# FFN down product as seven half-size block products, with operand sums formed in the up stage

## The chip, the cores and the metric

The kernel runs on one core of a Trainium2 chip. The metric is the time of the whole kernel on the device in microseconds. The engines of the core are named as in the profile: PE (TensorE, the matrix engine; PEld is its loading of the stationary operand), DVE (VectorE), ACT (ScalarE), POOL (GpSimd) and SP (SyncE, which here issues nearly all DMA transfers).

## The reference

One decoder layer on 1024 tokens and 16 prepended meta tokens, model width 1024. Behind two token mixers comes the feed-forward part, which this change is about. Cut to what matters:

```python
D_MODEL, SEQ, D_FF, FFN_TAPS = 1024, 1024, 2816, 3

h = layer_norm(DEEPNORM_ALPHA * h + mixed @ w_out, ln1_g, ln1_b)
up = causal_dwconv(h @ ffn_w_up, ffn_dw, ffn_dw_b)
u, g = jnp.split(up, 2, axis=-1)
f = (jax.nn.gelu(g, approximate=False) * u) @ ffn_w_down
return layer_norm(DEEPNORM_ALPHA * h + f, ln2_g, ln2_b)
```

Everything is in float32. The last product, the down product, takes the 1024 x 2816 result of the gate and the 2816 x 1024 weight `ffn_w_down`.

## The kernel before, in words

**Precision.** Every matrix operand is split into a rounded part `hi` (a cast on ScalarE, line 1042, 317 or 1203) and the rest `lo` (a subtraction on VectorE, line 1043, 320 or 1204). A product is three matmuls: hi x hi, hi x lo, lo x hi. The stationary operand is 128x128, the moving one up to 512 columns wide, and the result goes to one of eight PSUM banks.

**Up stage (about 664 to 1084 us).** It runs over `FC` = 22 chunks of 128 gate channels and the 128 value channels that belong to them. Each turn already uses seven block products in place of eight for the product with `w_up` (line 1139): names B11, B21, BT2, BT4, BT1, BT3 and B22, 24 matmuls each, into four double banks `pw`, `px`, `pz`, `py`. The sums on the activation side stand in memory for the whole stage; the sums on the weight side are formed per turn (lines 1064 to 1070) and split into a ring of ten slots (`RING`), up to nine products ahead (`w_ahead(9)`). The results leave PSUM by copies on ScalarE (line 1151) and additions on VectorE (line 1147): `c11` from `pz`, `c22` and `c21` behind the sixth product, `c12` from `py` behind the seventh. `u13`, `u2` and `c22` are work rows in `OB`. Then come the convolution of three taps (lines 1100 to 1102), the gelu and the product of gate and value (line 1110). The 128x1024 result of a turn is stored to DRAM as `fd[c]`, in two halves of 512 tokens.

**Down stage (from 1084 us).** It loads `fd` and `w_down` back, splits them, and multiplies: two passes over 512 tokens each, all 22 chunks of 128 in a pass, in blocks of 2, then 4 chunks; in a block four row tiles of 128 tokens and two halves of 512 output columns, three matmuls per chunk (line 1239). The eight banks of a pass accumulate over the whole pass. The weight is loaded and split once per pass. Landing places: eight ring slots in `FA` (`ftmp`) for `fd`, two buffers `wr` for the weight. In block 14 the residual rows are loaded from `h1d` and prepared (lines 1228 and 1229). With the last block each row tile gets its two banks added (line 1242), then the layer norm: statistics (229, 233), square root on ScalarE (236), a few one-column steps (237 to 245), scaling (1249, 1250) and two stores to the output.

**What sets the order.** Instructions of an engine run in the order of its queue. A scheduler writes the queues: `rank(p)` sets an instruction's priority (lower goes first), `after(a, b)` puts `a` behind `b` in the queue, and waits between engines come from the data. Transfers issued with `load` stand in SP's queue in order; a transfer that must wait for its data holds up those behind it.

Of the kernel before, what the change touches and what calls it, by code (L numbers as in the profile page):

```python
# [29 lines left out]
P = 128  # L30
# [14 lines left out]
FC = DFF // P  # L45
NB = S // P
# [52 lines left out]
def tile_hybrid_layer(  # L99
# [55 lines left out]


# [61 lines left out]
    def ln_stats(srcs, pool=None, tag="", bufs=4, behind=None):  # L218
# [7 lines left out]
        for j, (src, m) in enumerate(srcs):  # L226
            st = small.tile([P, 2, 6], F, name="st")
            for i in range(2):
                ins = nc.vector.bn_stats(st[:m, i, :], src[:, i * 512:(i + 1) * 512])
# [562 lines left out]
    RX = rx_p.tile([P, 4096], R, name="RX")  # L792
# [235 lines left out]
    ps_stack.close()  # L1028
    up_stack = ExitStack()
# [79 lines left out]
    def f_out(c, h, gate, t):  # L1109
        nc.vector.tensor_tensor(t, t, gate, OP.mult)  # L1110
        load(fd[c, :, h * 512:(h + 1) * 512], t)

    last_mm, copied = [], []
    RK_CHAIN = 400
    with rank(RK_SPLIT):
        w_ahead(7)
    for c in range(FC):
        V4, X, Z, Y = (pup.tile([P, 1024], F, name=n, tag=n) for n in ("pw", "px", "pz", "py"))
        passes = ((1,), (0,)) if c == 0 else ((0, 1),)
        for subs in passes:  # L1120
# [24 lines left out]
            def tt(*x):  # L1145
                with rank(RK_CHAIN):
                    nc.vector.tensor_tensor(*x)
# [7 lines left out]
            prod(B21, Z, True)  # L1155
            tt(c11[:, a:b], at(Z), u13[:, a:b], OP.add)
# [13 lines left out]
            tt(c22[:, a:b], c22[:, a:b], u13[:, a:b], OP.add)  # L1170
# [14 lines left out]
    g1, b1, g2, b2_ = (dn.tile([P, D], F, name=n) for n in ("g1", "b1", "g2", "b2"))  # L1185
    for i, t in enumerate((g1, b1)):
        load(t, dram(ln1_in, i * D, [[0, P], [1, D]]))
    for i, t in enumerate((g2, b2_)):
        load(t, dram(ln2_in, i * D, [[0, P], [1, D]]))
    nc.vector.tensor_scalar(b1, b1, ALPHA, None, OP.mult)  # L1190

    w_dn_v = w_down.rearrange("(k p) c -> k p c", p=P)
    FS = [(RX, i * 1024) for i in range(4)] + [(RHO, i * 1024) for i in range(8)]
    WS = [(t, i * 2048) for t in (OC, RHC) for i in range(4)]
    fs_n, wd_n = [0], [0]

    def f_chunk(c, s):
        raw = ftmp()
        load(raw, fd[c, :, s * 512:(s + 1) * 512])
        t, o = FS[fs_n[0] % len(FS)]  # L1200
        fs_n[0] += 1
        hi, lo = t[:, o:o + 512], t[:, o + 512:o + 1024]
        nc.scalar.copy(hi, raw)
        nc.vector.tensor_tensor(lo, raw, f32(hi), OP.subtract)  # L1204
        return hi, lo

    def wd_chunk(c):
        raw = wraw([P, D])
        load(raw, w_dn_v[c])
        t, o = WS[wd_n[0] % len(WS)]  # L1210
        wd_n[0] += 1
        hi, lo = t[:, o:o + 1024], t[:, o + 1024:o + 2048]
        split(raw, hi, lo, True)
        return hi, lo

    BLOCKS = [range(0, 2)] + [range(a, a + 4) for a in range(2, FC, 4)]
    BANKS = (2, 3, 4, 5, 0, 1, 6, 7)
    for s in range(2):
        banks = [pdn.tile([P, 512], F, name="ps_d", tag=f"d{j}") for j in range(8)]
        rows = []  # L1220
        for cs in BLOCKS:
            ops = [f_chunk(c, s) + wd_chunk(c) for c in cs]
            first, last = cs[0] == 0, cs[-1] == FC - 1
            if cs[0] == 14:
                for i in range(4):
                    r = dn.tile([P, D], F, name="r", tag="r", bufs=4)
                    load(r, h1d[(s * 4 + i) * P:(s * 4 + i + 1) * P, :])
                    nc.vector.scalar_tensor_tensor(r, r, ALPHA, g1, OP.mult, OP.mult)
                    nc.vector.tensor_tensor(r, r, b1, OP.add)
                    rows.append(r)  # L1230
# [74 lines left out]
```

## Time and profile before

| | us |
|---|---|
| three runs, median (lowest, highest) | 1341.49 (1341.06, 1342.19) |
| the profiled execution's own time | 1339.96 |
| its span, first to last instruction | 1338.1 |
| up stage, from the first full turn | about 664 to 1083.9 |
| down stage on TensorE | 1083.87 to 1327.94 |
| from TensorE's last matmul to the end | 10.16 |

The page gives the busy time of each engine and its share of the span. A window row gives the same for a stretch. A timeline row is one or several equal instructions: start, length, engine, line, what is written and read, and in brackets how long the engine stood idle before and what ended that. A group row is all instructions of one line and shape: busy time, mean nanoseconds of one, idle time in front of them and its releasers. Durations of neighbours on an engine overlap a little, so the distance of starts is shorter than the duration. L12 is line 12 of the kernel that the row belongs to; the change shifts lines, so the same instruction has other numbers before and after.

### The profile page before, as it was taken

How to read it: one execution, taken by the hardware profiler on the slowest of the kernel's cores; microseconds unless marked ns; L12 is line 12 of the kernel's file. 1: busy time of each engine (PE TensorE's matmuls, PEld its weight loads, DVE VectorE, ACT ScalarE, POOL GpSimd, SP SyncE). 2: the span in 40 equal slices, each digit the busy share in tenths (PEclk: the TensorE clock that was granted, in tenths of full speed). 3: DMA queues.
4: the chain of work that ended last, by engine and by line, in shares of the span. 5: the costliest groups of instructions: out<-in, count | busy, mean ns of one | idle time of the engine just before them, and what ended most of it. 6: DMA issues, size and time to landing. Idle time of an engine off the chain costs nothing.

```text
span 1338.1 us, 21743 instructions
## 1 busy us (share of the span) xinstructions
PE 1305.2 (98%) x8646; PEld 1215.2 (91%) x8646; DVE 1015.0 (76%) x1759; ACT 574.0 (43%) x1047; POOL 70.0 (5%) x43
## 2 busy tenths in 40 slices
PE   6999999999999999999899999999999999999996
PEld 5999999999999999878899999999999988888885
DVE  8689899999969576466988778778778784468417
ACT  4522244545473223344655555555555553323310
POOL 1300000010112231000000000000000000000000
PEclk9999999999999999999899999999999999999999
DMA  8363633333146553312221221221221296437311
GB/s 306 102 215 96 161 92 106 87 89 100 63 128 175 173 150 103 110 48 95 80 95 64 80 95 64 80 96 66 78 95 66 93 351 215 173 135 235 120 46 63
DMA packets 73769, 160.14 MB, mean 120 GB/s; under 512 B 9284, under 2 KB 34436, under 8 KB 73411
## 3 DMA queue, kind: packets, MB, share of 16 engines
q1 hardware_dynamic: 61898, 147.67, 34.6%
q10 hardware_dynamic: 11768, 11.08, 2.5%
q8 instruction: 68, 1.11, 0.3%
q14 instruction: 35, 0.28, 0.1%
HBM read 121.39 MB, written 39.63 MB: 120 GB/s over the span
## 4 chain that ended last, share of the span: by engine, by line
PE 92%; DVE 3%; DMA 2%; ACT 2%; issue 1%; SPq 0%; ACTq 0%; DVEq 0%
PE ps_d L1239 18%; PE px L1139 13%; PE py L1139 9%; PE ps_z L343 8%; PE ps_z L342 8%; PE ps_z L344 8%; PE pw L1139 5%; PE pz L1139 4%; PE ps_p L343 2%; PE ps_p L344 2%; PE ps_p L342 2%; PE ps_w L342 2%; PE ps_w L344 2%; PE ps_w L343 2%; PE ps_t L640 1%; PE ps_s L616 1%
## 5 line engine op out<-in xcount | busy, mean ns | idle before, releaser
L461 DVE SCALAR_TENSOR_TENSOR FA<-cin,cols,FA 128x1026 f32<-128x1026 f32 x120 | 155.4, 1307 | 0.2
L342 PE MATMUL ps_z<-RHO,whi 128*128 128x384 f32 (+3 forms) x360 | 116.2, 325 | 3.4 <-DVE cin L452 2.8
L343 PE MATMUL ps_z<-RHO,whi 128*128 128x384 f32 (+3 forms) x360 | 117.0, 325 | 0.0
L344 PE MATMUL ps_z<-RHO,wlo 128*128 128x384 f32 (+3 forms) x360 | 116.8, 325 | 0.0
L343 PE MATMUL ps_z<-RHC,whi 128*128 128x384 f32 (+3 forms) x360 | 116.7, 324 | 0.0
L342 PE MATMUL ps_z<-RHC,whi 128*128 128x384 f32 (+3 forms) x360 | 116.6, 324 | 0.0
L344 PE MATMUL ps_z<-RHC,wlo 128*128 128x384 f32 (+3 forms) x360 | 116.3, 323 | 0.0
L1043 DVE TENSOR_TENSOR RHO<-wr,RHO 128x512 fp32r<-128x512 f32 x94 | 63.8, 689 | 43.7 <-ACT RHO L1042 43.7
L1239 PE MATMUL ps_d<-OC,RHO 128*128 128x512 f32 x384 | 94.7, 395 | 0.0
L1239 PEld LDWEIGHTS ps_d<-OC,RHO 128*128 128x128 f32 x384 | 72.0, 188 | 17.3
L1042 ACT CAST RHO<-wr 128x512 fp32r<-128x512 f32 x94 | 57.2, 620 | 66.6 <-PE pz L1139 23.0
L342 PEld LDWEIGHTS ps_z<-RHO,whi 128*128 128x128 f32 x360 | 68.2, 190 | 4.0 <-DVE cin L452 3.0
L1239 PE MATMUL ps_d<-RHC,RHO 128*128 128x512 f32 x288 | 69.5, 391 | 0.0
L344 PEld LDWEIGHTS ps_z<-RHO,wlo 128*128 128x128 f32 x360 | 68.4, 190 | 1.1 <-issue 0.7
L343 PEld LDWEIGHTS ps_z<-RHO,whi 128*128 128x128 f32 x360 | 68.3, 190 | 0.6 <-issue 0.2
L344 PEld LDWEIGHTS ps_z<-RHC,wlo 128*128 128x128 f32 x360 | 68.1, 189 | 0.3
L343 PEld LDWEIGHTS ps_z<-RHC,whi 128*128 128x128 f32 x360 | 68.0, 189 | 0.4 <-issue 0.2
L317 ACT CAST whi<-wr 128x1024 fp32r<-128x1024 f32 x40 | 42.0, 1049 | 61.4 <-PE ps_z L343 42.7
L342 PEld LDWEIGHTS ps_z<-RHC,whi 128*128 128x128 f32 x360 | 67.9, 189 | 0.4 <-issue 0.2
L1239 PEld LDWEIGHTS ps_d<-RHC,RHO 128*128 128x128 f32 x288 | 54.0, 188 | 12.3 <-DVE RHO L1204 0.5
L320 DVE TENSOR_TENSOR OC<-wr,OC 128x1024 fp32r<-128x1024 f32 x24 | 29.3, 1223 | 30.5 <-ACT OC L317 30.4
L468 ACT ACTIVATE FA<-ps_z,cols 128x386 f32<-128x386 f32 (+2 forms) x48 | 26.0, 542 | 60.1 <-PE ps_z L344 57.2
(374 smaller groups left out, 3359.7 us busy)
## 6 DMA issues: line engine op xcount, KB each, us to landing
wr<-in_w_up_dram SPq DMA_DIRECT2D x44, 512.0 KB, 3.2
wr<-in_w_down_dram SPq DMA_DIRECT2D x44, 512.0 KB, 3.5
wr<-in_w_z_dram SPq DMA_DIRECT2D x30, 512.0 KB, 3.8
fd<-FA SPq DMA_DIRECT2D x44, 256.0 KB, 2.0
FA<-fd SPq DMA_DIRECT2D x44, 256.0 KB, 4.2
qt<-qd SPq DMA_DIRECT2D x28, 256.0 KB, 4.1
OB<-sgd SPq DMA_DIRECT2D x21, 256.0 KB, 3.5
x<-in_x_dram SPq DMA_DIRECT2D x8, 512.0 KB, 8.7
```

The lines of the kernel that those rows point to most:

```text
L317: ins = nc.scalar.copy(hi, raw)
L320: return (nc.vector if quick else nc.gpsimd).tensor_tensor(lo, raw, f32(hi), OP.subtract)
L342: nc.tensor.matmul(ps, ah, bh, start=i == 0, stop=False)
L343: nc.tensor.matmul(ps, ah, bl, start=False, stop=False)
L344: nc.tensor.matmul(ps, al, bh, start=False, stop=i == n - 1)
L461: nc.vector.scalar_tensor_tensor(acc[c], cin[:, j:j + U], wc, acc[c], OP.mult, OP.add)
L468: nc.scalar.activation(t, ps, AF.Tanh, bias=bcol(14 + i), scale=0.5)
L616: nc.tensor.matmul(ps[:, :w], qh[:, r], keys, start=True, stop=False)
L1042: nc.scalar.copy(hi, src)
L1043: ins = nc.vector.tensor_tensor(lo, src, f32(hi), OP.subtract)
L1139: ins = nc.tensor.matmul(o, x[:, ks], bmat(sub, q, hl, k), start=first and k + j == 0, stop=k == 3 and j == 2, skip_group_check=not first)
L1239: nc.tensor.matmul(ps, x[:, ts], y[:, hs], start=first and j + k == 0, stop=last and j == len(ops) - 1 and k == 2)
```

## The change

The down product is cut into halves: tokens (512 and 512), channels (`FH` = 11 chunks and 11 chunks) and output columns (512 and 512). A11, A12, A21 and A22 are the blocks of the gate's result, B11 to B22 those of `w_down`. Seven products of half size replace eight:

- sums: S1 = A21 + A22, S2 = S1 - A11, S3 = A11 - A21, S4 = A12 - S2; T1 = B12 - B11, T2 = B22 - T1, T3 = B22 - B12, T4 = T2 - B21;
- products, in this order: A22 T4, A11 B11, S1 T1, S2 T2, S3 T3, S4 B22, A12 B21.

The products go to two sets of four banks, `ps_z` and `ps_x`. S2 T2 and S3 T3 accumulate on top of A11 B11 or of what stands there by then, and S4 B22 on top of S1 T1, so that the banks are read in between, and 32 additions of 128x512 bring them into the eight row tiles, which now start from the residual rows (loaded in halves, one or two per step, during the first three products).

The sums are formed in the up stage, one chunk pair per turn in turns 1 to 11 (T, from `w_down`) and 13 to 21 (S, from `fd` chunks of earlier turns): two 512 KB loads (`sums_load`), four additions of 128x512 (`sums_form`), two 512 KB stores to the DRAM tensors `td` and `sd`. The last two S sums are formed during the first two products. The down stage then loads each operand of a product in pairs of chunks (128x2x512), from `fd`, `w_down`, `td` or `sd`, and splits it; six pairs (the last a single chunk) make a product, and up to six pairs stand ready (`d_ahead`). The last product runs its last five pairs row tile by row tile. `RX` is cut from 4096 to 2064 columns to make room for the landing places `raw` and `sums`.

```diff
+FH = FC // 2
+    td, sd = (dpool.tile([FH, P, 4 * 512], F, name=n) for n in ("td", "sd"))
...
-    RX = rx_p.tile([P, 4096], R, name="RX")
+    RX = rx_p.tile([P, 2064], R, name="RX")
...
+    sums_p = ctx.enter_context(tc.tile_pool(name="sums", bufs=1, side="right", reuse_waits="tile"))
+    RXF, SM1 = (sums_p.tile([P, 2048], F, name=n) for n in ("raw", "sums"))
+    SM = [[t[:, h * 1024:(h + 1) * 1024] for h in range(2)] for t in (OB[:, 2048:4096], SM1)]
+    SM = [SM[i % 2] for i in range(FC)]
+    def sums_load(i):
+        t, j = SM[i], i % FH
+        for h in range(2):
+            after(load(t[h], (w_dn_v if i < FH else fd)[j + h * FH]),
+                  loads[-1] if loads else f_stores[-1])
+    def sums_form(i, behind=None):
+        t, j = SM[i], i % FH
+        tt = nc.vector.tensor_tensor
+        x11, x12, x21, x22 = (x[:, q:q + 512] for x in t for q in (0, 512))
+        if i < FH:
+            ins = tt(x11, x12, x11, OP.subtract)
+            tt(x12, x22, x12, OP.subtract)
+            tt(x22, x22, x11, OP.subtract)
+            tt(x21, x22, x21, OP.subtract)
+        else:
...
+        after(ins, behind)
+        for h in range(2):
+            load((td if i < FH else sd)[j, :, h * 1024:(h + 1) * 1024], t[h])
...
             prod(B21, Z, True)
+            if last and c not in (0, FH + 1):
+                sums_load(c - 1 if c <= FH else c - 2)
...
-            tt(c22[:, a:b], c22[:, a:b], u13[:, a:b], OP.add)
+            ins = tt(c22[:, a:b], c22[:, a:b], u13[:, a:b], OP.add)
+            if last and c not in (0, FH + 1):
+                sums_form(c - 1 if c <= FH else c - 2, ins)
             tt(c21[:, a:b], u13[:, a:b], at(V4), OP.subtract)
...
+    X, Z = ([pdn.tile([P, 512], F, name=f"ps_{n}", tag=f"d{j}") for j in b]
+            for n, b in (("x", (0, 1, 6, 7)), ("z", (2, 3, 4, 5))))
+    F_AT = [(RHC, 6144), (RX, 0), (RHC, 2048), (RHO, 0), (RHO, 2048), (RHO, 4096)]
+    W_DN = [(OC, 0), (OC, 2048), (OC, 4096), (OC, 6144), (RHC, 0), (RHC, 4096), (RHO, 6144)]
+    F_RAW = [RXF[:, 0:1024], RXF[:, 1024:2048]] + [FA[:, i * 1024:(i + 1) * 1024] for i in range(6)]
+    W_RAW = [None, None] + [OB[:, i * 1024:(i + 1) * 1024] for i in (2, 3, 0, 1)]
+    PAIRS = [(j, min(2, FH - j)) for j in range(0, FH, 2)]
...
+    def operand(i, src, j, n, raws, places):
+        raw = raws[i % len(raws)]
...
+        ins = load(raw.rearrange("p (n c) -> p n c", c=512), src(j, n))
...
+        nc.scalar.copy(hi, raw)
+        los.append(nc.vector.tensor_tensor(lo, raw, f32(hi), OP.subtract))
+        if len(los) > 1:
+            after(los[-1], evacs.pop() if evacs else los[-2])
+        return hi, lo
...
+        for f, w in ((A22, T4), (A11, B11_), (S1, T1), (S2, T2), (S3, T3), (S4, B22_), (A12, B21_)):
+            for j, n in PAIRS:
+                yield (n,) + operand(i, f, j, n, F_RAW, F_AT) + operand(i, w, j, n, W_RAW, W_DN)
+                i += 1
...
+    def down(banks, first, done, by_tile=0, same=False):
+        def mms(i, pairs, a, z):
+            ops = [(p, c * 512) for p in pairs for c in range(p[0])]
+            for x, ((n, fh, fl, wh, wl), o) in enumerate(ops):
+                ts, ws = slice(o + i * P, o + i * P + P), slice(o, o + 512)
+                for k, (l, r) in enumerate(((fh, wh), (fh, wl), (fl, wh))):
+                    nc.tensor.matmul(banks[i], l[:, ts], r[:, ws], start=first and a and x + k == 0,
+                                     stop=z and x == len(ops) - 1 and k == 2, skip_group_check=not first)
+        n = len(PAIRS) - by_tile
+        for y in range(n):
+            p = d_next(y < 3 or not same)
+            for i in range(4):
+                mms(i, [p], y == 0, y == len(PAIRS) - 1)
+            if extra:
+                extra.pop(0)()
+        last = [d_next() for _ in range(by_tile)]
+        for i in range(4):
+            if last:
+                mms(i, last, n == 0, True)
+            with rank(RK_EVAC):
+                ins = done(i)
...
+    def add(t, half, bank, op=OP.add, full=False):
+        r = rows[t][:, half * 512:half * 512 + 512]
+        ins = nc.vector.tensor_tensor(r, r, bank, op)
+        if full:
+            nc.vector.bn_stats(stats[t][:, half], r)
+        return ins
...
+    down(Z, True, lambda i: add(4 + i, 0, Z[i], OP.subtract))
+    down(X, True, lambda i: add(i, 0, X[i]))
+    down(Z, True, lambda i: add(4 + i, 1, Z[i]))
+    down(X, False, lambda i: add(i, 1, X[i]), same=True)
+    down(X, False, u3)
+    down(Z, False, lambda i: add(i, 1, Z[i], full=True))
+    down(X, True, c11_, 5)
```

`extra` is a list of steps, one per pair of the first three products: the last two sets of sums, the rows of gains and the halves of the residual rows. `u3` adds the fifth product to both halves of rows 4 to 7 and finishes them; `c11_` adds the last one to rows 0 to 3 and finishes them.

More of the change, by code (lines that the diff above doesn't have):

```diff
@@ L226, in ln_stats @@
         for j, (src, m) in enumerate(srcs):
-            st = small.tile([P, 2, 6], F, name="st")
-            for i in range(2):
+            st = half_stats or small.tile([P, 2, 6], F, name="st")
+            for i in range(0 if half_stats is None else 2, 2):
                 ins = nc.vector.bn_stats(st[:m, i, :], src[:, i * 512:(i + 1) * 512])
@@ L1184, in tile_hybrid_layer @@
     pdn = ctx.enter_context(tc.tile_pool(name="pdn", bufs=1, space=PSUM, reuse_waits="tile"))
[L1185 to L1202, printed above, removed]
+    X, Z = ([pdn.tile([P, 512], F, name=f"ps_{n}", tag=f"d{j}") for j in b]
+            for n, b in (("x", (0, 1, 6, 7)), ("z", (2, 3, 4, 5))))
+    def blk(t, first, step, col):
+        return lambda j, n: dram(t, (first + j) * P * step + col, [[step, P], [P * step, n], [1, 512]])
@@ new lines, in tile_hybrid_layer, with ln_rows, gain_rows @@
+    rows, stats = {}, {}
+    extra = []
+    def ln_rows(names):
+        return [wsp_p.tile([P, D], F, name=n, tag=t) for n, t in zip(names, ("whi", "wlo"))]
+    gains = ln_rows(("g1", "b1"))
+    g1, b1 = gains
+    SM[FC - 2] = ln_rows(("s1", "s2"))
+    def gain_rows(i):
+        for t in range(2):
+            after(load(gains[2 * i + t], dram((ln1_in, ln2_in)[i], t * D, [[0, P], [1, D]])), loads[-1])
+        if i == 0:
+            nc.vector.tensor_scalar(b1, b1, ALPHA, None, OP.mult)
@@ new lines, in residual_row, with do @@
+    def residual_row(i, half):
+        if i not in rows:
+            rows[i] = dn.tile([P, D], F, name=f"r{i}")
+            stats[i] = dn.tile([P, 2, 6], F, name=f"st{i}")
+        hs = slice(half * 512, half * 512 + 512)
+        r = rows[i][:, hs]
+        after(load(r, h1d[i * P:(i + 1) * P, hs]), loads[-1])
+        after(nc.vector.scalar_tensor_tensor(r, r, ALPHA, g1[:, hs], OP.mult, OP.mult), los[-1])
+        nc.vector.tensor_tensor(r, r, b1[:, hs], OP.add)
+    def do(f, *x):
+        extra.append(lambda: f(*x))
@@ new lines, in add, with norm_out @@
+    def add(t, half, bank, op=OP.add, full=False):
[4 more added lines that the diff above has]
+        return ins
+    def norm_out(t):
+        r, (g2, b2_) = rows[t], gains[2:]
+        (mu, rs), = ln_stats([(r, P)], half_stats=stats[t])
+        for half in range(2):
+            hs = slice(half * 512, half * 512 + 512)
+            a = r[:, hs]
+            nc.vector.scalar_tensor_tensor(a, a, mu, g2[:, hs], OP.subtract, OP.mult)
+            nc.vector.scalar_tensor_tensor(a, a, rs, b2_[:, hs], OP.mult, OP.add)
+            load(out[0, t * P:(t + 1) * P, hs], a)
```

115 lines of the change are left out of this document (66 added, 49 removed).

## The prediction, as it was made before the result was known

> **What bounds the kernel now.** I read the page first: the busy times, then the shares of the chain that ended last.
>
> ```profile
> PE 1305.2 (98%) x8646; PEld 1215.2 (91%) x8646; DVE 1015.0 (76%) x1759; ACT 574.0 (43%) x1047; POOL 70.0 (5%) x43
> ...
> PE 92%; DVE 3%; DMA 2%; ACT 2%; issue 1%; SPq 0%; ACTq 0%; DVEq 0%
> ```
>
> TensorE is busy for 98% of the span and carries 92% of the chain. A busy share is an average, so I asked next for the two stages that the change touches, by windows: a piece of the up stage, then the down stage in three pieces and its tail.
>
> ```profile
> 960.00:1060.00 100.00, 100.00 (x843) 100.00 (x843) 78.61 (x125) 52.06 (x84) 0.00 (x0) 1.00 0.24 80
> ```
> ```profile
> 1083.87:1107.31 23.44, 23.41 (x103) 18.98 (x102) 22.64 (x28) 9.23 (x13) 0.00 (x0) 1.00 0.95 359
> 1107.31:1205.00 97.69, 97.69 (x421) 79.04 (x422) 48.48 (x74) 31.52 (x42) 0.00 (x0) 1.00 0.51 174
> 1205.00:1327.94 122.94, 122.93 (x534) 99.73 (x532) 64.69 (x101) 26.10 (x36) 0.00 (x0) 1.00 0.34 116
> 1327.94:1338.10 10.16, 0.00 (x0) 0.00 (x0) 6.87 (x17) 0.30 (x1) 0.00 (x0) 0.70 0.28 103
> ```
>
> The columns are length, busy time and count of PE, PEld, DVE, ACT and POOL, then granted clock, DMA share and GB/s. TensorE has no gap in either stage, at a granted clock of 1.00; VectorE is busy for 79% of the up stage. Even the first piece of the down stage, at 359 GB/s and a DMA share of 0.95, left TensorE 23.41 us of 23.44. The chain in order of time gives the stages' ends and the period of the up loop.
>
> ```profile
> 906.85 2.85 PE pz L1139 x24
> ...
> 926.84 2.87 PE pz L1139 x24
> ...
> 1083.87 23.41 PE ps_d L1239 x103
> 1107.31 220.63 PE ps_d L1239 x953
> ```
>
> One turn of the up loop takes 926.84 - 906.85 = 20.0 us: 7 products of 24 matmuls of 258 or 256 columns, 119 ns each. The down stage runs from 1083.87 to 1327.94, 244.07 us for 1056 matmuls of 512 columns, 231.1 ns each. Twice the columns cost nearly twice the time, so a matmul left out there is worth its full 231 ns as long as its operands arrive.
>
> **What is removed on TensorE.** Before: 22 chunks x 8 row tiles x 2 halves x 3 = 1056 matmuls. After: 7 products x 11 chunks x 4 row tiles x 3 = 924, of the same shape. 132 x 231.1 ns = **30.5 us** off the path. At the rates of the first and second piece (23.44/103 = 228 ns, 97.69/421 = 232 ns) it is 30.1 to 30.6; were all 924 at 228 ns, the stage would be 33.4 us shorter.
>
> The Trainium skill, "TensorE: Matmul & The Clock Gate", section "Back-to-back issue gap", speaks against this size: it gives about 131 ns per matmul of 512 columns in a stream of weight loads and matmuls. By it the 132 would be worth 17.3 us. This trace does not agree (231.1 ns), and the trace decides.
>
> **What is added in the up stage.** Twenty of the 22 turns load two 128x1024 tiles, form four sums of 128x512 on VectorE and store two tiles. The price of a sum is read off VectorE's timeline in one turn.
>
> ```profile
> 947.22 0.69 DVE L1064 TENSOR_TENSOR wr<-wr 128x512 f32<-128x512 f32 x1
> 947.83 0.75 DVE L1101 SCALAR_TENSOR_TENSOR FA<-OB,cols,FA 128x512 f32<-128x512 f32 x1
> ...
> 956.63 0.69 DVE L1043 TENSOR_TENSOR RHO<-wr,RHO 128x512 fp32r<-128x512 f32 x1
> 959.53 0.69 DVE L1043 TENSOR_TENSOR RHO<-wr,RHO 128x512 fp32r<-128x512 f32 x1 [2.21 <-ACT RHO L1042]
> 961.74 0.69 DVE L1043 TENSOR_TENSOR RHO<-wr,RHO 128x512 fp32r<-128x512 f32 x1 [1.51 <-ACT RHO L1042]
> 962.35 0.69 DVE L1147 TENSOR_TENSOR OB<-OB 128x514 f32<-128x514 f32 x1
> ...
> 964.08 0.69 DVE L1147 TENSOR_TENSOR OB<-py,FA 128x514 f32<-128x514 f32 x1 [0.45 <-PE py L1139]
> ```
>
> A sum of this shape lasts 0.69 us, but the next instruction starts 0.61 us after it. Four cost 2.4 us by starts, 2.8 by durations. A turn holds 78.61 / 5 = 15.7 us of VectorE work, so 18.1 to 18.5 of 20.0. The Trainium skill, "VectorE: DVE Perf Modes", section "The TRN2 errata", has the per-instruction latency exposed between instructions and 691 ns for such an add; by it the four cost 2.8 us. The duration agrees and the spacing (0.61) does not.
>
> Does the rest fit? VectorE's idle time in a turn is 2.21 + 1.51 + 0.45 = 4.2 us here, nearly all of it before weight splits that wait for ScalarE, and these casts wait in turn:
>
> ```profile
> L1042 ACT CAST RHO<-wr 128x512 fp32r<-128x512 f32 x94 | 57.2, 620 | 66.6 <-PE pz L1139 23.0
> ```
>
> They wait for TensorE to give a ring slot back. Such a wait is slack: if VectorE comes later, it waits less. The ring's ten slots hold the weights some eight products (8 x 2.86 = 23 us) ahead. VectorE's rows from the `c21` addition of turn 17 on, before:
>
> ```order
> L1147 TENSOR_TENSOR FA<-OB,pw 128x514
> L1147 TENSOR_TENSOR OB<-py,FA 128x514
> L1101 SCALAR_TENSOR_TENSOR FA<-OB,cols,FA 128x512
> L1043 TENSOR_TENSOR wlo<-wr,wlo 128x512
> L1101 SCALAR_TENSOR_TENSOR FA<-FA,cols 128x512
> L1102 SCALAR_TENSOR_TENSOR FA<-OB,cols,FA 128x512
> ```
>
> and now (lines 1188, 1108, 1109 and 1050 are the old 1147, 1101, 1102 and 1043; 1147 to 1149 are sums):
>
> ```order
> L1188 TENSOR_TENSOR FA<-OB,pw 128x514
> L1147 TENSOR_TENSOR sums<-sums 128x512
> L1108 SCALAR_TENSOR_TENSOR FA<-OB,cols,FA 128x512
> L1148 TENSOR_TENSOR sums<-sums 128x512
> L1188 TENSOR_TENSOR OB<-py,FA 128x514
> L1108 SCALAR_TENSOR_TENSOR FA<-FA,cols 128x512
> L1109 SCALAR_TENSOR_TENSOR FA<-OB,cols,FA 128x512
> L1050 TENSOR_TENSOR RHO<-wr,RHO 128x512
> L1149 TENSOR_TENSOR sums<-sums 128x512
> ```
>
> The sums stand behind the additions `c22` and `c21`, so `u13`, which the next copy out of PSUM overwrites, is free as early as before. Only the `c12` addition (bank `py`, next written four products or 11 us later) comes two or three instructions later. I take the up stage at nothing. The first sum also waits for its loads, with the `c12` addition queued behind it; they are issued behind the `fd` stores of the turn before:
>
> ```profile
> 951.74 2.13 SPq L110 DMA_DIRECT2D fd<-FA  x2
> ```
>
> Those end at 953.87, the `c22` addition comes at 962.35; with the stores some 2.4 us later, 6 us are left, and a load lands in 3.2 us (below). If the sum waits anyway, the cover is the 11 us and the ring. DMA adds 4 x 512 KB per turn, 105 GB/s on top of 80; the piece at 174 GB/s above held nobody up. On SP the stores of the sums wait for VectorE and hold the `fd` stores and the next loads behind them, which have a turn's time.
>
> **The passage from up to down.** Pairs 0 and 1 of the first product are split in the last turn. From pair 4 on, the loads stand on SP behind the last turn's stores. Around these stores there stood before:
>
> ```order
> L110 DMA wr<-in_w_down_dram 128x1024
> L110 DMA FA<-fd 128x512 x3
> L110 DMA wr<-in_w_down_dram 128x1024
> L110 DMA fd<-FA 128x512
> L110 DMA FA<-fd 128x512 x2
> L110 DMA fd<-FA 128x512
> L110 DMA FA<-fd 128x512 x2
> ```
>
> and now (`td`, `sd`: the sums in DRAM; `raw` and `FA`: landing places of chunk pairs):
>
> ```order
> L111 DMA sd<-sums 128x1024 x2
> L111 DMA fd<-FA 128x512 x2
> L111 DMA FA<-fd 128x2x512
> L111 DMA OB<-td 128x2x512
> L111 DMA FA<-fd 128x512
> L111 DMA OB<-td 128x512
> L111 DMA s_11581<-fd 128x1024
> ```
>
> Before, loads went ahead of the last two `fd` stores and between them; now the loads of pairs 4 and 5 stand behind both, and behind the stores of sums. The prices of the splits and of landing:
>
> ```profile
> L320 DVE TENSOR_TENSOR RHC<-wr,RHC 128x1024 fp32r<-128x1024 f32 x20 | 24.5, 1226 | 12.0 <-ACT RHC L317 12.0
> L317 ACT CAST RHC<-wr 128x1024 fp32r<-128x1024 f32 x19 | 20.0, 1051 | 33.9 <-DMA wr<-in_w_down_dram 31.8 <-PE ps_d L1239 2.2
> ...
> L1242 DVE TENSOR_TENSOR r<-ps_d,r 128x512 f32<-128x512 f32 x16 | 11.0, 684 | 20.2 <-PE ps_d L1239 20.0
> ```
> ```profile
> FA<-fd SPq DMA_DIRECT2D x11, 256.0 KB, 4.1
> ...
> wr<-in_w_down_dram SPq DMA_DIRECT2D x4, 512.0 KB, 9.0
> ```
> ```profile
> wr<-in_w_up_dram SPq DMA_DIRECT2D x8, 512.0 KB, 3.2
> ```
>
> The last number is the us to landing: 4.1 and 9.0 at the crowded start of the down stage, 3.2 in the up stage. Between the last `c22` addition (2 us before the up stage's end, as now) and the multiplication that feeds the last `fd` store, VectorE has 15 rows of 512 columns (0.63) and 4 of 1024 (1.2): 14 us, so the store leaves 12 us into the down stage. Pair 4 then lands at 16 to 21, and with a cast (1.05) and two splits (1.2 each) is ready at 19.6 to 24.6; TensorE wants it after four pairs of 24 matmuls, 22.2 us. So 0 to 2.4 us of stall; pair 5, behind the store's landing, may add as much. I take **1.0 us**, nearer to the 4.1, since SP has held the queue empty until then; the ends are 0 and 5. Behind that the lead grows: a pair costs TensorE 5.5 us, and ScalarE 2.1 and VectorE 2.5.
>
> **The rest of the down stage.** VectorE's other groups there:
>
> ```profile
> L1204 DVE TENSOR_TENSOR RHO<-FA,RHO 128x512 fp32r<-128x512 f32 x28 | 18.6, 686 | 29.0 <-PE ps_d L1239 18.1 <-ACT RHO L1203 10.9
> ...
> L1249 DVE SCALAR_TENSOR_TENSOR r<-r,mv,g 128x512 f32<-128x512 f32 x16 | 11.3, 747 | 0.0
> L1250 DVE SCALAR_TENSOR_TENSOR r<-r,sd,b 128x512 f32<-128x512 f32 x16 | 11.2, 744 | 0.1
> L229 DVE BATCH_NORM_STATS2 st<-r 128x6 f32<-128x512 f32 x16 | 11.0, 689 | 0.1
> ```
>
> Now: splits, 14 operands x (5 x 1.23 + 0.69) = 96 us; additions, 32 instead of 16 at 0.68 = 22; 16 residual half rows x (0.75 + 0.69) = 23; the last two sets of sums, 5.5; scaling 22.5 and statistics 11 as before. Together 180 us of 213, hidden by TensorE. The fifth product writes on in the banks of the fourth: its first matmul into a bank comes 9 x 0.23 = 2.1 us after that bank's last, and the addition between takes 0.69: nothing, or about 1 us if VectorE is late.
>
> **The tail.** Behind TensorE's last matmul, before:
>
> ```profile
> 1327.96 0.69 DVE L1242 TENSOR_TENSOR r<-ps_d,r 128x512 f32<-128x512 f32 x1 [0.32 <-PE ps_d L1239]
> 1328.57 0.68 DVE L229 BATCH_NORM_STATS2 st<-r 128x6 f32<-128x512 f32 x1
> ...
> 1329.23 0.68 DVE L229 BATCH_NORM_STATS2 st<-r 128x6 f32<-128x512 f32 x1
> ...
> 1329.94 0.21 DVE L233 BATCH_NORM_AGGREGATE mv<-st 128x2 f32<-128x12 f32 x1
> 1330.07 1.36 DVE L1250 SCALAR_TENSOR_TENSOR r<-r,sd,b 128x512 f32<-128x512 f32 x2
> ...
> 1331.35 0.15 DVE L237 TENSOR_SCALAR sd<-mv 128x1 f32<-128x1 f32 x1
> ```
>
> One of the two statistics now comes earlier (0.6 us), and the tile before is done before the last matmul, since a tile's last five pairs last 27 x 0.23 = 6.2 us, so its scaling (1331.35 - 1330.15 = 1.2 us) leaves the chain: **1.8 us**, with ends 0.6 and 3.
>
> **Sum.** -30.5 - 1.8 + 1.0 = -31.3 us. The profiled execution took 1339.96 us (span 1338.1), 1.5 us under the median of 1341.49; from the median, 1341.49 - 31.3 = **1310.2 us**. With the best ends (-33.4, -3, 0) it is 1305; with the passage at 5 us and the tail at 0.6 it is 1315.
>
> **Rivals.** (1) *The down stage starves.* Loads, splits and sums crowd the first two products; if each lands 4.9 us later (9.0 for 4.1) than TensorE wants, 5 us go per product, 10 in all: 1313 to 1322. For it: the 9.0. Against it: what SP issues from pair 4 to the last pair of product 2 (6.5 pairs of 1 MB, 3 MB of sums and gains, 5 residual half rows) is about 11.8 MB, 33 us at 359 GB/s, and TensorE takes from 12 to 58 us of the down stage to get there. (2) *VectorE becomes the bound of the up stage.* If its 4.2 us of idle time stay and the sums come on top, a turn takes 22.4 to 22.8 us, and 20 turns cost 48 to 55: 1358 to 1366, slower than before. It decides from the point where more than 1.5 us of the idle time cannot be given up; the break-even lies at 31.3/20 = 1.6 us per turn, with 3.1 to 3.5 fixed. Against it speaks that the idle time ends with ring slots. A part of it (0.5 us per turn) gives 1320. (3) *Matmuls left out are not worth 231 ns*, because the stage waits for something else: at most the change gives nothing, 1341. TensorE's 100% speaks against that.
>
> **Chances.** Forecast 0.72 (1305 to 1314), rival 1 0.16, rival 2 in part 0.05 and in full 0.04, rival 3 0.02, better than 1304 0.01. A difference under 0.2% cannot be told from none here: faster 0.94, same 0.02, slower 0.04. The range 1304 to 1322 takes in the forecast's bounds and rival 1.
>
> **What would show it.** Down matmuls: 924 in 213 to 215 us with TensorE without gap; an up turn still 20.0 us with VectorE at 90 to 93%; VectorE's waits for ScalarE before splits shrunk to under 2 us per turn; a gap of TensorE, if any, at pair 4 or 5, 20 to 28 us into the down stage; a tail of about 8.4 us. Turns longer than 20.0 us, or TensorE waiting for splits through several products, would prove me wrong.

## The result, and the profile after

| | before | after |
|---|---|---|
| median of 4 runs, us | 1341.40 (1341.06 to 1342.19) | 1310.76 (1309.61 to 1311.61) |
| ratio, with 95% interval | | 0.977 (0.9753 to 0.9787) |
| profiled execution, us (its span) | 1339.96 (1338.1) | 1310.53 (1308.7) |
| start of the steady up stage, us | 663.72 | 666.71 |
| up stage from there, us | 420.0 | 420.1 |
| down stage to TensorE's last matmul, us | 244.2 | 213.6 |
| behind TensorE's last matmul, us | 10.16 | 8.32 |
| from the start of the up stage to the end, us | 674.4 | 642.0 |

The forecast was 1310.2 us. The start of the up stage is here the first `px<-RHC,wlo` matmul of the turns; its row in the timeline of after (the four parts of a row: start, duration, what, and in brackets the idle time before it) is

```profile
666.71 1.73 PE L1180 MATMUL px<-RHC,wlo 128*128 128x258 f32 x12 [0.27 <-ACT OB L1192]
```

The same row stood at 663.72 before. These 3.0 us lie ahead of all work that the change adds or leaves out (only the layout of memory is changed there, and that is tried by itself below), and further down they turn out to vary from execution to execution. So stages are compared by their own lengths here.

**The down stage.** The chain of waits of after, from the last up product on (start, duration, engine, tile and line, and behind the x the number of instructions):

```profile
1084.10 2.87 PE py L1180 x24
1086.97 30.49 PE ps_z L1299 x132
1117.46 30.49 PE ps_x L1299 x132
1147.94 30.64 PE ps_z L1299 x132
1178.59 60.97 PE ps_x L1299 x264
1239.56 30.32 PE ps_z L1299 x132
1269.88 30.50 PE ps_x L1299 x132
1300.37 0.02 issue
1300.39 0.70 DVE r L1368
...
1301.12 0.70 DVE st L1370
...
1302.24 1.32 DVE r L1379 x2
```

Seven products, 924 matmuls, one behind the other from 1086.97 to 1300.37 with no piece of another engine between them: 213.40 us, 231.0 ns for each (the table's 213.6 count from the first row of the timeline, at 1086.81). Behind the last one stands one statistic (`st`) where the chain before had two, and one pair of scalings less.

**The passage.** In the timeline of after, the last two stores of `fd` leave SP's queue (SPq) between 1094.19 and 1099.18 (two issues in one row). The load of pair 4, the fifth pair of the first product, stands behind them at 1100.91. Its operand from `fd` is cast when it lands, 3.6 us later, and split at 1105.61; the weight sum is split at 1107.53. The row of TensorE that needs them starts at 1109.11; the last two rows are the weight's split of pair 6, the first of the second product, and TensorE's row of that pair:

```profile
1094.19 4.99 SPq L111 DMA_DIRECT2D fd<-FA  x2
1100.91 0.37 SPq L111 DMA_DIRECT2D FA<-fd  x1
...
1104.53 1.05 ACT L1261 CAST RHO<-FA 128x1024 fp32r<-128x1024 f32 x1 [6.77 <-DMA FA<-fd]
...
1105.61 1.23 DVE L1262 TENSOR_TENSOR RHO<-FA,RHO 128x1024 fp32r<-128x1024 f32 x1 [6.78 <-ACT RHO L1261]
...
1107.53 1.23 DVE L1262 TENSOR_TENSOR RHC<-OB,RHC 128x1024 fp32r<-128x1024 f32 x1 [0.69 <-ACT RHC L1261]
...
1109.11 1.09 PE L1299 MATMUL ps_z<-RHC,RHO 128*128 128x512 f32 x4
...
1114.87 1.23 DVE L1262 TENSOR_TENSOR RHO<-wr,RHO 128x1024 fp32r<-128x1024 f32 x1
...
1117.30 5.61 PE L1299 MATMUL ps_x<-RHO,RHC 128*128 128x512 f32 x24
```

By these rows pair 4 is ready at 1107.53 + 1.23 = 1108.76, 0.35 us ahead of its use; no idle time stands in brackets at the matmul. Pair 6 is ready at 1116.10, 1.2 us ahead. Read in the same way, pair 5 is 4.7 us ahead, and pairs 7 to 11 are 1.4, 1.6, 2.5, 4.6 and 7.2 us ahead. So the lead is short at pair 4 and again through the first half of the second product, and grows only behind that. The DMA engines were as crowded as the first rival said. The transfers of 1087 to 1150: the GB/s in 40 slices of 1.6 us, their total, and name, count, size and us to landing of two groups:

```profile
GB/s 407 406 398 304 148 376 1 0 166 77 375 282 298 415 401 403 411 401 385 388 388 391 382 388 382 390 402 407 385 390 386 386 390 388 415 388 399 407 368 74
DMA packets 9881, 21.34 MB, mean 339 GB/s; under 512 B 768, under 2 KB 768, under 8 KB 9877
...
FA<-fd SPq DMA_DIRECT2D x4, 512.0 KB, 8.6
...
OB<-in_w_down_dram SPq DMA_DIRECT2D x3, 512.0 KB, 10.0
```

The long hole, 0 to 166 GB/s in the seventh to tenth slice (1096 to 1103), is the time in which SP waits for the last `fd` data and for their store.

**The up stage.** Two stretches of 100 us, five turns each (TensorE, weight loads, VectorE, ScalarE, GpSimd, then granted clock, DMA share and GB/s), and the two waits of VectorE between 700 and 1080 that the argument turns on (total, number, longest):

```profile
760.00:860.00 100.00, 100.00 (x842) 100.00 (x842) 90.62 (x145) 51.21 (x85) 0.00 (x0) 1.00 0.51 186
...
960.00:1060.00 100.00, 100.00 (x842) 100.00 (x842) 91.11 (x147) 51.52 (x86) 0.00 (x0) 1.00 0.52 184
```
```profile
DVE OB L1188 <- ACT OB L1192: 22.5, 19, 3.2
...
DVE RHO L1050 <- ACT RHO L1049: 7.1, 11, 0.8
```

TensorE is never idle, with 842 matmul records in each stretch (844 and 843 before), and VectorE went from 79% to 91%. Its wait for ScalarE's cast ahead of a split into `RHO` fell from 41.6 us to 7.1 (with `whi` and `wlo`, the other places of the ring, from 66.7 to 11.8); a wait of 1.2 us per turn ahead of the `c22` addition is new.

### The profile page after: what moved, and what is told of

Read it like the earlier page. It is cut to its first block, busy times and chain, and to the rows that moved or that the text cites. A ratio compares the mean times of both kernels' runs of the same rounds, so it can differ in the third digit from the quotient of the medians.

```text
span 1308.7 us, 21696 instructions
## 1 busy us (share of the span) xinstructions
PE 1277.3 (98%) x8514; PEld 1193.2 (91%) x8514; DVE 1089.4 (83%) x1875; ACT 580.5 (44%) x1043; POOL 69.8 (5%) x43
## 4 chain that ended last, share of the span: by engine, by line
PE 91%; DVE 4%; ACT 2%; DMA 2%; issue 1%; SPq 0%; ACTq 0%; DVEq 0%
PE px L1180 14%; PE py L1180 9%; PE ps_x L1299 9%; PE ps_z L346 8%; PE ps_z L347 8%; PE ps_z L345 8%; PE ps_z L1299 7%; PE pw L1180 5%; PE pz L1180 5%; PE ps_p L346 2%; PE ps_p L347 2%; PE ps_p L345 2%; PE ps_w L345 2%; PE ps_w L346 2%; PE ps_w L347 2%; PE ps_t L643 1%
## 5 line engine op out<-in xcount | busy, mean ns | idle before, releaser
L323 POOL TENSOR_TENSOR wlo<-wr,whi 128x1024 fp32r<-128x1024 f32 x17 | 41.5, 2442 | 191.1 <-ACT whi L320 176.6
L1192 ACT COPY FA<-px 128x514 f32<-128x514 f32 (+2 forms) x23 | 13.1, 570 | 83.0 <-PE px L1180 82.9
L1180 PE MATMUL px<-OA,RHO 128*128 128x258 f32 x324 | 44.9, 288 | 2.9 <-ACT OA L926 1.8
L1180 PEld LDWEIGHTS px<-OA,RHO 128*128 128x128 f32 x324 | 41.8, 194 | 3.4 <-ACT OA L926 2.0
L1107 ACT ACTIVATE FA<-OB,cols 128x512 f32<-128x512 f32 x44 | 35.9, 815 | 18.4 <-DVE OB L1188 18.4
```

Source lines behind the costliest of these rows:

```text
L323: return (nc.vector if quick else nc.gpsimd).tensor_tensor(lo, raw, f32(hi), OP.subtract)
L1107: nc.scalar.activation(t, cc[:, 2:HW], AF.Identity, bias=ffw(3, o), scale=ffw(2, o))
L1180: ins = nc.tensor.matmul(o, x[:, ks], bmat(sub, q, hl, k), start=first and k + j == 0, stop=k == 3 and j == 2, skip_group_check=not first)
```

## The experiments

The theory: TensorE sets the pace of both stages, so the time falls by what the left-out matmuls take (30.5 us) and by the shorter tail, while the sums fit into VectorE's idle time and the lead of prepared pairs carries TensorE over the passage. The rivals: the down stage starves for operands, VectorE sets the up stage's turn, or a matmul left out is not worth 231 ns. All kernels, by the trace of one profiled execution (us) and by their runs. The experiments ran in three groups, each with the kernel before beside it; its medians there were 1340.1 to 1341.2 us, so that medians of different groups can be compared to about 1 us:

| kernel | up stage | down stage | behind it | from up start to end | median of runs, us |
|---|---|---|---|---|---|
| before | 420.0 | 244.2 | 10.16 | 674.4 | 1341.4 |
| after | 420.1 | 213.6 | 8.32 | 642.0 | 1310.8 |
| e8_layout_only | 420.3 | 244.4 | 10.13 | 674.9 | 1341.8 |
| e1_sums_old_down | 420.1 | 250.5 | 10.20 | 680.8 | 1349.1 |
| e1b_no_late_sums | 420.3 | 244.7 | 10.14 | 675.1 | 1342.0 |
| e2_no_sums | 420.3 | 213.6 | 8.35 | 642.2 | 1309.9 |
| e3_2_more_adds | 424.6 | 214.5 | 8.34 | 647.4 | 1314.1 |
| e3_4_more_adds | 434.2 | 219.1 | 8.36 | 661.6 | 1330.3 |
| e3_8_more_adds | 470.5 | 220.1 | 8.42 | 699.0 | 1364.2 |
| e4_third_product_two_thirds | 420.5 | 206.1 | 8.42 | 635.0 | 1302.4 |
| e5_passage_loads | 420.3 | 213.6 | 8.47 | 642.4 | 1311.1 |
| e5b_loads_behind_stores | 420.7 | 219.0 | 8.48 | 648.1 | 1314.9 |
| e6_last_product_untiled | 420.6 | 213.6 | 18.35 | 652.5 | 1317.1 |

### The layout alone

The kernel before with the changed kernel's places in memory (a smaller `RX`, `RW` beside it, the DRAM tiles for the sums), nothing computed:

```diff
-    RX = rx_p.tile([P, 4096], R, name="RX")
+    RX = rx_p.tile([P, 2064], R, name="RX")
...
+    RW = wo_stack.enter_context(tc.tile_pool(name="rw", bufs=1, side="right", reuse_waits="tile")).tile(
+        [P, 2048], R, name="RW")
```

> The kernel before with only the new layout of memory: RX cut to 2064 columns, its other half in a place of its own that is freed after the output projection, the two more DRAM tensors declared; no sums, old down product. Theory (the 3.0 us by which the changed kernel's profiled execution reaches the up stage later are differences from execution to execution in the first 200 us): 1341.4 us within 1.5. Rival (the layout makes the stages ahead of the up loop slower): 1343.5 to 1344.5 us, with the first full turn of the up loop near 666.7 us in the profile instead of 663.7.

Measured: 1341.8 us (1339.65 to 1346.18), ratio 1.0005 (0.9994 to 1.0015). The places cost and gain nothing that can be measured.

### The sums without the new product

The changed kernel's up stage, with 20 sets of sums formed and stored that nobody reads, ahead of the old down product:

```diff
+            if last and c not in (0, FH + 1):
+                sums_load(c - 1 if c <= FH else c - 2)
...
+                sums_form(c - 1 if c <= FH else c - 2, ins)
```

> The sums are loaded, formed and stored in turns 1 to 11 and 13 to 21 of the up stage, and the down product is the old one of 1056 matmuls, which reads none of them. Theory (the sums lie in VectorE's slack): a turn stays at 20.0 us with VectorE at 18.1 us of it, and the time is that of before, 1341.4 us within 1.5. Rival (the sums cost time on the path, and part of the new down product's gain pays for it): 0.1 us per turn and more, 1343.5 us or above; with the waits of VectorE all fixed, 2.4 us per turn, about 1390 us.

Measured: 1349.08 us (1347.84 to 1350.06), ratio 1.0055 (1.0042 to 1.0069). My theory expected no difference: a miss. The time lies in the rival's range (1343.5 us or above), but not for the rival's reason, a cost in each turn: the table puts the loss in the down stage (250.5 for 244.2) and nothing in the up stage. The timeline of this kernel has TensorE waiting twice, 23 and 32 us into the down stage (in brackets), and its windows show the first 40 us:

```profile
1108.84 5.74 PE L1284 MATMUL ps_d<-RHC,RHO 128*128 128x512 f32 x24 [0.90 <-ACT RHO L1248]
1117.77 8.72 PE L1284 MATMUL ps_d<-RHC,RHO 128*128 128x512 f32 x30 [3.19 <-ACT RHO L1248]
```
```profile
1085.57:1105.00 19.43, 19.43 (x87) 15.79 (x86) 19.43 (x26) 7.82 (x12) 0.00 (x0) 1.00 1.03 406
1105.00:1126.00 21.00, 16.91 (x66) 13.11 (x65) 15.68 (x20) 11.10 (x15) 0.00 (x0) 0.92 0.93 337
```

The sums of the last turns put VectorE at 19.43 of 19.43 us and the DMA engines at 406 GB/s just when the old down stage fetches its first blocks (before, its first 23.4 us had VectorE at 22.6 us and 359 GB/s), and the granted clock is 0.92 in the stretch of the waits. The chain of waits that leads to the second gap shows what came late; its longest pieces are transfers of `fd`:

```profile
1091.23 9.90 DMA FA<-fd
...
1101.15 6.99 DMA FA<-fd
...
1111.60 5.47 DMA FA<-fd
```

These are 22.4 us of transfers, and 2.0 us of VectorE's splits stand between them. The next kernel leaves out the last four turns' sums alone:

```diff
-            if last and c not in (0, FH + 1):
+            if last and c not in (0, FH + 1) and c < 18:
```

> The kernel with the old down product and the sums formed in the up stage, but now without the sums of the last four turns, so that no sum's transfer lies near the passage (the sums that are formed are read by nobody; the result is unchanged). With all sums it took 1349.1 us. Theory (the 8 us were lost at the passage, where the sums' loads and stores stood in the way of the down stage's first loads; the sums of the turns before cost nothing): 1341.4 us within 1.5, with no gap of TensorE longer than in the kernel before. Rival (the sums cost time wherever they are, by VectorE's or the queue's work in every turn): 18 of 22 turns keep their share, about 1347 to 1348 us.

Measured: 1341.97 us (1340.01 to 1342.64), ratio 1.0004 (0.9995 to 1.0013). The first kernel's 8 us went with four of 20 sets, as the theory said. The sums cost only where they meet the passage. By the chain above the transfers came late there. How much VectorE's fuller queue added, by giving landing places back later, no run separates: sums and transfers went together.

### The new product without the sums

The changed kernel with plain blocks of `fd` and `w_down` read in the place of all sums; so its output is not the layer's, but the matmuls, splits and operand loads of the down stage are the same in number and size (the last two sets of sums, formed in the down stage, are left out too):

```diff
-    T1, T3, T4, T2 = (blk(td, 0, 2048, q * 512) for q in range(4))
-    S2, S3, S4, S1 = (blk(sd, 0, 2048, q * 512) for q in range(4))
+    T1, T3, T4, T2 = B12_, B22_, B21_, B11_
+    S2, S3, S4, S1 = A11, A21, A12, A22
```

> No sums are formed, loaded or stored; the seven products take plain blocks of the two matrices in place of the sums, so the output is another one; everything else of the changed kernel stays, 924 matmuls. Theory: the same time as the changed kernel, 1310.8 us within 1.5, and VectorE back at about 15.7 us per turn. Rival (the sums cost something): faster by what they cost, 1308 us or below.

Measured: 1309.94 us (1308.22 to 1311.82), ratio to before 0.9764 (0.9747 to 0.978), against 0.977 for after. VectorE is back at 79% in the up stage:

```profile
760.00:860.00 100.00, 100.00 (x843) 100.00 (x842) 79.20 (x125) 52.63 (x86) 0.00 (x0) 1.00 0.23 80
```

From the up stage's start to the end it takes 642.2 us, after 642.0. All sums together, with their 20 x 4 transfers of 512 KB in the up stage (184 for 80 GB/s in its windows), cost nothing that can be measured in the new kernel.

### How far VectorE is from setting the turn

Two, four and eight more operations of 512 columns per turn (a maximum of a block with itself, which changes nothing), in 20 turns:

```diff
+        for k in range(2 if i < FC - 2 else 0):
+            u = (x11, x12, x21, x22)[k % 4]
+            tt(u, u, u, OP.max)
```

> The changed kernel with eight more VectorE operations of 128x512 per turn behind the four sums (each leaves its operand as it is). VectorE then needs 18.1 + 8 x 0.61 = 23.0 us of a turn of 20.0. Theory: VectorE is the bound of the up stage; turns take 23.0 us once the lead of the weight ring (up to 23 us) is used up, so 20 turns cost 60 us less at most 23: 1348 to 1371 us. Rival (VectorE's idle time in front of the splits cannot be given up): 20 x 8 x 0.61 = 98 us more, 1408 us.

> The changed kernel with two more additions of 512 columns on VectorE in each of 20 turns of the up stage (a maximum of a sum's block with itself, which changes nothing in the result): 1.2 us more per turn. Theory (VectorE's 1.8 us of idle time per turn are ring slots and can be given up; TensorE sets the turn until VectorE has 20 us of work): turns of 20.0 us, VectorE at 96 to 97%, 1310.8 us within 1.5. Rival (a part of the idle time is fixed waits, 1 us per turn or more): 0.4 to 1.2 us per turn, 1319 to 1335 us.

> As e3_2_more_adds with four more additions per turn, 2.4 us: VectorE then has 20.6 us of work in a turn. Theory (VectorE sets the turn from 20 us on, with the 2% idle that it kept under eight more): turns of 20.6 to 21.0 us, 12 to 20 us in all, 1318 to 1331 us; by a straight line to the 53 us of eight more additions from a break at 1.8 us, 11 us, 1322 us. Rival (fixed waits of 1.8 us per turn come on top): 2.4 us per turn, 1359 us.

Measured: two 1314.05 us (ratio to before 0.9804, 0.9789 to 0.9819), four 1330.26 us (0.9922, 0.9896 to 0.9948), eight 1364.18 us (1.0168, 1.0154 to 1.0182). The up stage grew by 4.5, 14.1 and 50.4 us, or 0.2, 0.7 and 2.5 us per turn for 1.2, 2.4 and 4.9 us of added work at 0.61 us each, from start to start. Eight and four lie in the theory's ranges. Two lies between theory and rival: the turn was expected to stay at 20.0 us, and it lengthened by 0.2. In the down stage these kernels lose 0.9, 5.5 and 6.5 us on top (table), so that the work added to the last turns costs at the passage too. The windows of the kernels with two (first row) and eight more show how TensorE loses its full share while VectorE fills:

```profile
760.00:860.00 100.00, 98.64 (x829) 98.42 (x828) 94.83 (x153) 52.01 (x85) 0.00 (x0) 1.00 0.50 178
```
```profile
760.00:860.00 100.00, 92.88 (x743) 92.25 (x742) 99.62 (x162) 45.22 (x75) 0.00 (x0) 0.95 0.45 154
```

In the kernel with two more, the 0.2 us are an average that hides the way it happens. TensorE waits in three turns only, near 813, 914 and 1056 us, each time for VectorE's split of an up weight (total, number, longest); in before and after it waits for no split in these turns. A wait of ScalarE for the up weights' loads has become long too:

```profile
PE px L1183 <- DVE RHO L1050: 2.8, 2, 1.4
PE px L1183 <- DVE whi L1050: 0.8, 1, 0.8
```
```profile
ACT RHO L1049 <- DMA wr<-in_w_up_dram: 27.5, 19, 3.3
```

TensorE's waits are 3.6 of the 4.5 us. The chain that leads to each of them runs over VectorE's own rows, one behind the other for some 9 us (additions, sums, convolution, splits), and no transfer is in it, so the later loads of the up weights are not what these waits come from. So 1.2 us of VectorE's 1.8 us of idle time per turn can be used at a small price; less than that was not tried.

### What a matmul left out is worth

The third product without its matmuls of low by high part (44 of 132):

```diff
-                for k, (l, r) in enumerate(((fh, wh), (fh, wl), (fl, wh))):
+                for k, (l, r) in enumerate(((fh, wh), (fh, wl), (fl, wh))[:terms[0]]):
...
+    terms[0] = 2
```

> The changed kernel with the matmuls of low by high part left out in the third of the seven products (132 becomes 88; so that product is computed less exactly), everything else as it was. Theory (TensorE sets the pace in the whole down stage, a matmul left out is worth 231 ns): 44 x 0.231 = 10.2 us less, 1300.6 us within 1, if the operands of the products behind still arrive in time; the lead there is 2 to 10 us by the records, so a part, at most 3 us, may be lost to waits in the fourth product. By the 131 ns that the Trainium skill (TensorE: Matmul & The Clock Gate, Back-to-back issue gap) gives for a matmul of 512 columns it would be 5.8 us less, 1305.0 us. Rival (the operands set the pace, the matmuls only fill the time): 1310.8 us.

Measured: 1302.36 us (1300.85 to 1305.65), ratio to before 0.9713 (0.9696 to 0.9729): 8.4 us under after, where the theory allowed 7 to 11. The down stage is 7.5 us shorter (206.1 for 213.6). The difference to 10.2 is in the timeline of TensorE, at the start of the fourth product:

```profile
1156.64 9.50 PE L1299 MATMUL ps_z<-OC,RHO 128*128 128x512 f32 x40
1167.22 1.19 PE L1299 MATMUL ps_x<-RHC 128*128 128x512 f32 x4 [1.09 <-ACT RHC L1261]
1169.53 4.84 PE L1299 MATMUL ps_x<-RHC 128*128 128x512 f32 x20 [1.12 <-DVE RHC L1262]
```

The third product ends at 1166.1, its operands' pace was set for 30.5 us per product, and the first 24 matmuls of the next one end at 1174.2 where 1171.7 would be 24 x 0.231 later: 2.5 us of waiting. 10.2 - 2.5 = 7.7, against 7.5. So a matmul is worth its 231 ns as long as operands are ahead, and the lead at that place (7.3 us in after, where the first pair of the fourth product is ready at 1171.17 and used at 1178.43) is used up when a product runs 10 us faster. The 131 ns that the Trainium skill (TensorE: Matmul & The Clock Gate, Back-to-back issue gap) gives for a matmul of 512 columns would give at most 5.8 us; the trace does not agree, and the measured 7.5 decides.

### How much the passage can bear

Four transfers of 512 KB that nobody needs (from `w_down` to a spare place in DRAM), ahead of pair 4's loads in the queue; in the first kernel they may go before the last stores of `fd`, in the second they stand behind them:

```diff
+        if i == 4 and not more:
+            for k in range(4):
+                more.append(load(spare[k], w_dn_v[k]))
-                after(more[-1], loads[-1])
+                after(more[-1], loads[-1] if k else f_stores[-1])
+                loads.append(more[-1])
```

> The changed kernel with four more transfers of 512 KB put into SP's queue ahead of the loads of pair 4 at the passage into the down stage (they copy up-weight-sized blocks of w_down to a spare place in DRAM that nobody reads; the result is unchanged). Theory (the passage stands on the lead of four prepared pairs, and pair 4 was ready only 0.4 us before TensorE wanted it): the 2 MB, at the 339 to 390 GB/s that the engines move there, take 5 to 6 us, pair 4 comes that much later, and TensorE stands still for 5 to 6 us once, about 21 us into the down stage; 1315 to 1318 us (up to 1322 if a copy inside DRAM costs twice). Rival (the lead is not what decides; the queue has slack that the records of one execution do not show): 1310.8 us within 1, and no gap of TensorE.

> As e5_passage_loads, but the four transfers of 512 KB now stand in SP's queue behind the last two stores of fd and directly ahead of pair 4's loads; in e5 they stood ahead of the stores, and left in a stretch in which the DMA engines had nothing to do (pair 4's load was issued 15.05 us into the down stage, 13.94 without them). The result is unchanged. Theory (pair 4's lead is 0.4 us, counted from the store of fd that its data wait for; what stands behind that store delays it in full): 2 MB at 339 to 390 GB/s are 5.4 to 6.2 us, so TensorE stands still for 4 to 6 us about 22 us into the down stage, 1315 to 1317 us. Rival (the lead is larger than the records say, or the extra transfers and pair 4's share the engines so that pair 4 loses little): under 1.5 us, 1310 to 1312 us.

Measured: 1311.13 us (ratio to before 0.9775, 0.976 to 0.9789) for the first, as after; the theory, 5 to 6 us, missed. 1314.85 us (0.981, 0.9795 to 0.9824) for the second, 4.1 us over after; its down stage took 5.4 us more (219.0), within the 4 to 6 us of the theory, though the time lies 0.15 us under its range. In SP's queue of the first kernel the four left at 1087.77, ahead of the stores:

```profile
1087.77 2.47 SPq L111 DMA_DIRECT2D spare<-in_w_down_dram  x4
1090.85 3.40 SPq L111 DMA_DIRECT2D sd<-sums  x2
1094.52 4.99 SPq L111 DMA_DIRECT2D fd<-FA  x2
1102.35 0.37 SPq L111 DMA_DIRECT2D FA<-fd  x1
```

In the second they left 9 us later, directly ahead of pair 4, and TensorE's row of pair 4 has the wait in brackets:

```profile
1096.96 2.49 SPq L111 DMA_DIRECT2D spare<-in_w_down_dram  x4
1099.56 0.51 SPq L111 DMA_DIRECT2D FA<-fd  x1
```
```profile
1101.24 5.75 PE L1305 MATMUL ps_z<-OC,RHO 128*128 128x512 f32 x24
1110.58 10.02 PE L1305 MATMUL ps_z<-RHC,RHO 128*128 128x512 f32 x36 [3.59 <-ACT RHC L1267]
```

Pair 4's load was issued 15.2 us into the down stage in the first kernel (first row at 1087.13) and 15.0 in the second (1084.54). What differs is what lay ahead of it in the DMA engines: VectorE began its first split of pair 4 at 1107.10 in the first (20.0 us in) and at 1109.05 in the second (24.5 us in). 3.59 us of waiting and 10.02 - 36 x 0.231 = 1.7 us more within the row make 5.3 of the 5.4. In the first kernel the same bytes moved ahead of SP's wait for VectorE's last results, and filled most of the hole that after has there. The GB/s from 1080 to 1125 in slices of 1.1 us, after (first row) and the first kernel; look at the 12th to 20th slice:

```profile
GB/s 291 197 273 186 390 397 408 408 404 391 406 204 113 395 220 0 0 189 44 40 346 364 273 282 377 408 404 406 406 411 404 382 388 390 388 386 395 371 397 384
```
```profile
GB/s 235 228 277 182 357 415 408 408 402 381 670 452 415 437 153 393 426 337 195 11 15 246 395 282 268 306 408 413 402 399 410 408 395 388 384 391 386 382 386 382
```

The first kernel also shows how long the lead of after was. Pair 4 came 1.2 us later into the stage here (its first split 20.0 us in, after 18.8), and the split of its weight ended at 1109.00 + 1.22 = 1110.22, 0.8 us behind the start of TensorE's row of pair 4 (1109.44). Of the three matmuls of a chunk the first takes rounded parts alone, so the row can begin before the split is done. TensorE's loading of stationary operands did wait for this split:

```profile
PEld ps_z L1305 <- DVE RHC L1268: 0.2, 1, 0.2
```

Its product still took 30.51 us, after's 30.49. So 1.2 us of delay used up the lead and cost next to nothing: the lead of after was about 1 us by this, and 0.35 us by the rows of the two engines, which are not to be set against each other to better than that.

### The order of the last product

The last product pair by pair to its end, in place of its last five pairs row tile by row tile:

```diff
-    down(X, True, c11_, 5)
+    down(X, True, c11_)
```

> The changed kernel with the last product's matmuls in the plain order, pair by pair over all row tiles to its end, in place of its last five pairs tile by tile; the same matmuls, the same result. Theory (the tail is short because three of the four last tiles are finished beside TensorE): the four tiles' last rows become ready within the last 3 to 4 us, and VectorE needs about 4.4 to 4.8 us for each (additions, statistics, scaling), so the tail grows from 8.3 to 17 to 20 us: 1319 to 1323 us. Rival (the finishing is not on the path; the tail is set by the last store's way out alone): 1310.8 us within 1.

Measured: 1317.12 us (1316.96 to 1321.05), ratio to before 0.9826 (0.981 to 0.9842), 6.4 us over after. The theory's 8 to 12 us were too many by the runs, not by the trace: the last product began at 1266.55 and took 30.5 us, so TensorE's last matmul ended at 1297.05 and the span at 1315.4, a tail of 18.35 us where after has 8.32, 10.0 more. Its up stage began at 662.89, 3.8 us earlier than after's, which is the difference. The window behind the last matmul shows VectorE as the one engine with work:

```profile
1297.05:1315.40 18.35, 0.00 (x0) 0.00 (x0) 15.28 (x45) 1.18 (x4) 0.00 (x0) 0.59 0.30 114
```

## Why the prediction was right, point by point

**The matmuls (-30.5).** Measured -30.6 (244.2 to 213.6). The price per matmul, taken from the old product, held in the new one (231.0 ns) and held for 44 more in the kernel with a shortened third product. The third rival is out.

**The sums in the up stage (0).** Measured +0.1; taking them away gives nothing back. The reason given held: VectorE's idle time ahead of the splits was a ring that was full, and it shrank from 66.7 us to 11.8. What the prediction did not see is the new wait ahead of `c22` (22.5 us), which is idle time too and costs nothing. The second rival needed more than 1.5 us of idle time per turn that cannot be given up. The runs put that part lower: 1.8 us per turn were left beside the sums, and 1.2 us more of work lengthened a turn by 0.2 us on average, which leaves about 0.8 us (an estimate, 1.8 - 1.2 + 0.2). The change as a whole would have been lost between 2.4 and 4.9 us of added work per turn (1330 and 1364 us, before 1341), by a straight line at 3.2 us.

**The passage (+1.0, ends 0 and 5).** Measured 0: the term was sized too high, within its ends. The parts came out as worked out: the last `fd` store left by 1099.18, 12.2 us into the down stage, where 12 us were said; pair 4's load from `fd` landed 3.6 us after its issue, near the 4.1 that were taken because the queue would be empty; pair 4 was ready 21.8 us in, where 19.6 to 24.6 were said; TensorE wanted it at 22.1, where 22.2 were said. One step was wrong, without a price here: "Behind that the lead grows". It was 4.7 us at pair 5, fell to 1.2 us at pair 6, stayed under 2 us up to pair 8, and grew only then. The sum of bytes against the first rival holds (11.8 MB come from seven pairs, not 6.5), but it compared totals over two products, and the lead was shortest at single pairs.

The mechanism of the first rival is real. Its landing times of 9 to 10 us are there; the old down stage lost 6.3 us when the sums were put ahead of it, with late transfers in the chain, and 2 MB more in the wrong place cost the new one 5.4. It did not come about because the lead, about 1 us at pair 4 and 1.2 us at pair 6, was just long enough. It was a near thing, and that it cost nothing at all is in part luck; the prediction gave the rival 0.16.

**The tail (-1.8).** Measured 10.16 to 8.32, -1.84. The row tile order of the last product is what makes it: without it the tail is 18.35 us.

**The sum.** -31.3 was forecast, and the stages give -30.6 + 0.1 - 1.84 = -32.3, from the up stage's start 674.4 to 642.0. The medians differ by 30.6, since what lies ahead of the up stage took 3.0 us more in the profiled execution of after. That the change does this is not shown, and three starts speak against it: the layout alone began its up stage at 664.23, and the two kernels with additional loads, which are the same up to the down stage, at 666.84 and 663.88. So the forecast of 1310.2 against 1310.76 is closer than its terms, by luck: 1.0 us too much at the passage and some 1.5 us of the stage ahead stand against each other.

## What to carry to other kernels

Where one engine runs without a gap, a change that takes work from it is worth that work at the price of its rows, and all else is a question of covers: list each cover with its length, and look for the shortest. Here the covers were VectorE's idle time (1.8 us per turn left, most of it usable) and the prepared pairs at the passage (about 1 us left at two places), and the second is where the same sums cost 6 us in front of another consumer. A cover has to be followed operand by operand: a total over a stage does not show where it is shortest. In these runs sums that were finished some turns ahead of the next stage cost nothing, and the same four transfers cost nothing ahead of the queue's wait for data and 5.4 us behind it.

## What was not expected of the hardware

- A 512 KB load took 3.2 us to land in the up stage of before and 8.6 to 10.0 us at the passage of after, where 339 GB/s were moved; most of that was queueing. Pair 4's load from `fd`, issued into an empty queue of after, landed in 3.6 us, and of the two kernels with the same four transfers, which issued it at the same point of the stage, one had it at VectorE 4.5 us later.
- Time ahead of the up stage varies by up to 4 us (starts at 662.89 to 666.84 in 13 profiled executions), so that differences of that size need the stage's own length.
- The granted clock fell in stretches in which TensorE had gaps: 0.92 in the 21 us of waits of the kernel with sums and old product, 0.95 to 0.98 in the up stage with eight more operations, 1.00 in after's up stage from 760 us on. Three single gaps of 0.8 to 1.4 us in the kernel with two more left it at 1.00 there.
